# ScalarE takes the second square of the MLP; a shorter warm-up, another queue for the first input tile, a halved last output, and new instruction orders

## The chip, the cores and the metric

The kernel runs on one NeuronCore of a Trainium2 chip. The metric is the device time of one execution in microseconds (us). The kernel before took 510.14 us, the median of three runs (510.87, 508.67 and 510.14).

## The reference

One step of a hybrid decoder layer over T = 320 tokens: a prompt of 256, and 8 samples with 8 new tokens each. The model width is 1024 and everything is in f32. The layer is a sum of three residual branches, each behind an rmsnorm:

```python
def layer(x, pos, k_past, v_past, conv_buf, h0, mem_k, mem_v, lp):
    hn = rmsnorm(x, lp['ln_mix_g'])
    proj = hn @ lp['w_in']
    ...
    att = moba_attention(q, k_all, v_all, pos).reshape(b, t, ATT_WIDTH)
    xbc_c, new_conv = causal_conv(xbc, conv_buf, lp['conv_w'], lp['conv_b'])
    ...
    y, h_new = ssd_scan(xs, dt, a, bm, cm, h0)
    y = gated_group_norm(y, z, lp['ssm_norm_g'])
    x = x + jnp.concatenate([att, y], axis=-1) @ lp['w_out']
    x = x + cross_attn(rmsnorm(x, lp['ln_x_g']), mem_k, mem_v, lp)
    hm = rmsnorm(x, lp['ln_mlp_g'])
    x = x + jnp.square(jax.nn.relu(hm @ lp['w_up'])) @ lp['w_down']
    return x, k, v, new_conv, h_new
```

Of these the change touches the start (the rmsnorm ahead of `w_in` and the first product), the MLP (`w_up` is 1024 x 4096, `w_down` 4096 x 1024), and the last piece of the output.

## The kernel before

**Products.** Every weight is streamed from HBM in chunks of 128 x 1024 f32. A chunk is loaded into `wr` (3 buffers; L341, a DMA issued on SyncE's queue, or on ScalarE's for some of the chunks), and split into two fp32r halves that TensorE can multiply: `wh`, a rounded copy made by ScalarE (L393), and `wl`, the rest, a subtraction on VectorE (L394); both have 3 buffers. The activations are split in the same way, and each product is three matmuls, high by high, low by high and high by low (`gemm3`, L399, L400, L401). So a chunk with eight tiles of 128 rows gives 24 matmuls of 128 x 320.

**Stages.** In-projection with QK-norm and rotary, paged attention, convolution and state-space scan, output projection; cross-attention to the memory; then the MLP, with 32 chunks of `w_up` (each makes one tile of the 4096 hidden rows) and 32 of `w_down` (four make one of the eight output tiles).

**Start.** GpSimd clears a zero tile `ts` (L544), on which TensorE does warm-up matmuls whose product nobody reads (L547; their widths are `NWARM`, L68, and each f32 matmul is two passes in the trace). The table `prm` (L346, on ScalarE's queue), the first tile of x (L344, SyncE) and the first half chunk of weights (L341, SyncE) are loaded meanwhile. `split` makes the two halves of each tile of x times the norm's gain in `prm`: ScalarE the high one (L539), VectorE the low one (L540). The first real product is L719.

**The MLP's hidden rows.** When the 24 matmuls of a hidden tile are done, `up_done` (L1687 to L1696) takes them out of PSUM: t = max(product, 0) times the norm's factor `rb` (VectorE, L1692), hh = t squared, rounded to fp32r (ScalarE, L1693), f = t squared in f32 (GpSimd, L1695), hl = f - hh (VectorE, L1696). `t` and `f` come from one pool of five buffers. The product lies in one of two PSUM buffers `mm`, which comes free when L1692 has read it; a few tiles at the start of the stage, before `rb` is there, lie in `as` too. The output tiles of the MLP are added to x2T on VectorE (L1355, in `residual`) and go out by a DMA on SyncE (L1739).

**Order.** Nothing is scheduled at run time. TensorE's order comes from the string ORDER, in which each letter lets one generator (a part of a stage) emit its next piece; V and F are parts of the start, `u` and `w` two groups of hidden tiles, `r` the MLP's norm factor. The orders of ScalarE, VectorE, GpSimd and of the DMAs are four lists of numbers, ACT_ORDER, DVE_ORDER, POOL_ORDER and DMA_ORDER (runs of indices into the program order), which `_issue_order` applies at the end. Each engine works through its own list strictly in order: an instruction that waits holds up all behind it on that engine.

Of the kernel before, what the change touches and what calls it, by code (L numbers as in the profile page):

```python
# [12 lines left out]
AF = mybir.ActivationFunctionType  # L13
ALU = mybir.AluOpType
# [6 lines left out]
T = TP + NB * TS  # L21
# [26 lines left out]
for _n, _c in (("g_mix", 8), ("g_x", 8), ("g_mem", 8), ("g_mlp", 8), ("g_ssm", 4),  # L48
# [16 lines left out]
AHEAD = 2000  # L65
AHEAD2 = 400
AHEAD3 = 600
NWARM = (512, 512, 352)  # L68
PACE = 1.3
ORDER = ("VFVVVQQQQQQQQQQQQQQVQFVQFQVFQFQQQFVQQQQSSQQQFSSQQQZQZSSFSFSVSSQFFBBBBSZBSZBBSFBBTBBSSSBBBSSBBTBTBBTS"  # L70
         "SBSBBSSBSSSBSTSTBZSZBBSSBTBBZBBTSDBZSSDSSSTSZSZDDZTDSSZSDDSDDSDTDZZDDSDSZDDSZRSSSSSRRSRRSMOOROWRRWOR"
         "OWNOOWNONOOOOOMOONNOOWNJJJJJJJJJJMJZJJWJJKJKKKKKKKKKKKKKKKWGGOGGMaXcGJMGGGGGMGWGGGGGGMXXbcXaabcadcbc"
         "babbXaaMbccdadcdddacdGGGGGGKGGGGGWGGGGGG!uuuwuruuuuwwrwwwwuwuuuuuuuuuuuuuuuuuuuutuuuuuuuutuuutuuuuuu"
         "uuuuuuutuuutuuuuutuuutututuuuuuuutuuuuutuuuuuuuuuutuuuttuuutuuutuuutuuuuuuuuuuuuuuuuuuuu")
ACT_ORDER = ("1+3 20 5+1 19 21 7 0 8+2 22 11+3 16+1 23 15 24 28 30 33 18 27 25 32 26 29 38 34 43 37 31 50 39 36 57 44 35 "
# [15 lines left out]
DVE_ORDER = ("0+3 17 4+1 18 6+1 9 8 19 10 12 14+1 13 11 20+1 27 32 25 22 26 35 23 28 16 30 36 31 29 51 24 33 37 34 39+1 38 "  # L91
# [19 lines left out]
DMA_ORDER = ("1+2 0 4+11 19+1 16+2 21+1 29+4 23 34+1 24 36 28 37+5 45 43 46 44 47+6 64 54 25+1 55+3 65 59+2 27 66 62 75 67+4 "  # L111
# [5 lines left out]
POOL_ORDER = ("13 0+1 3 5 8 4 7 11 2 6 12 18 9+1 14 26 15+2 25 19+2 23+1 22 28 27 46 29 32 31 30 35+1 47 34 37 33 44 38+2 42 "  # L117
              "45 43 49 41 48 50+1 53 52 54+31")
TAKEN = []


# [135 lines left out]
def _body(tc, nc, I, O):  # L257
    V, A, G, S, PE = nc.vector, nc.scalar, nc.gpsimd, nc.sync, nc.tensor
# [34 lines left out]
    def tm(n, dt=F32):  # L293
        return tl(tp_, [P, n], "t", dt, bufs=NT)
# [34 lines left out]
    xT, ay = xa[:, 0], xa[:, 1]  # L329
# [10 lines left out]
            c = HALVES[part] if part is not None else slice(0, 1024)  # L340
            last_load[:] = [(A if WSP <= i < WACT and ahead else S).dma_start(raws[i][:, c], I["w"][i][:, c]).ins]  # L341

    def load_x_tile(a, b):
        S.dma_start(xT[:, a:b, :], I["xT"][:, a:b, :])  # L344

    A.dma_start(prm[:, 0:8], I["prm"][:, 0:8])  # L346
    for kt in range(4):
        load_x_tile(kt, kt + 1)
        load(CH["v"] + kt // 2, False, kt % 2)
    load_x_tile(4, 6)  # L350
    load_x_tile(6, 8)
# [1336 lines left out]
    def up_done(m):  # L1688
        def done(ps):
            hh, hl = mlp["h"]  # L1690
            t = tm(T)
            V.scalar_tensor_tensor(t, ps[:, :T], 0.0, mlp["rb"], op0=ALU.max, op1=ALU.mult)  # L1692
            A.activation(hh[:, m, :], t, AF.Square)  # L1693
            f = tm(T)
            G.tensor_tensor(f, t, t, op=ALU.mult)  # L1695
            V.tensor_tensor(hl[:, m, :], f, hh[:, m, :], op=ALU.subtract)  # L1696
        return done

# [29 lines left out]
    xT = x2T[0]  # L1728
    hh, hl = mlp["h"]

    for m in range(8):
        ps = mm()
        for c in range(4):
            w = chunk(CH["dn"] + 4 * m + c)
            for k in range(8):
                kt = 8 * c + k
                gemm3(ps[:, :T], w, slice(k * P, k * P + P), hh[:, kt, :], hl[:, kt, :], kt == 0, kt == 31)
        residual(m, None, None, None)(ps)
        S.dma_start(O["yT"][:, m, :], xT[:, m, :])  # L1739
    for take, runs in ((lambda i: i.engine == mybir.EngineType.Activation, ACT_ORDER), (lambda i: i.engine == mybir.EngineType.DVE, DVE_ORDER),  # L1740
                       (lambda i: i.engine == mybir.EngineType.Pool, POOL_ORDER),
                       (lambda i: i.opcode == "DMACopy", DMA_ORDER)):
# [32 lines left out]
```

## Time and profile before

| | before |
|---|---|
| runs, us | 510.87, 508.67, 510.14; median 510.14 |
| the profiled execution's own time, us | 510.33 |
| its span, first to last instruction, us | 508.5 |
| PE busy, share of the span | 98% |
| DVE busy | 66% |
| ACT busy | 50% |
| POOL busy | 11% |
| mean granted TensorE clock | 1.00 |

Times in the profile count from the first instruction. PE is TensorE's matmuls, PEld its weight loads, DVE VectorE, ACT ScalarE, POOL GpSimd and SP SyncE. A row of the timeline gives start, duration, engine, line, operation, output<-inputs and the number of instructions; in square brackets stands how long the engine was idle before it and what released it. Rows with a q (ACTq, SPq) are the engine's own queue issuing a DMA. "xN" rows join N neighbours. Matmuls overlap in the array, so their durations (0.31 us for 128 x 320) are longer than the distance from start to start.

### The profile page before, as it was taken

The page shows a single profiled execution, that of the slowest core. Times are in us where ns is not written, and L with a number is a line of the kernel's source. Part 1 is how long each engine was busy: PE and PEld are TensorE (multiplying, and loading weights), DVE is VectorE, ACT ScalarE, POOL GpSimd, SP SyncE. Part 2 cuts the span into 40 slices and gives each one's busy share as a digit, 9 for nine tenths or more (in the row PEclk, how much of TensorE's full clock was granted, in tenths as well). Part 3 has the DMA queues.
Part 4 walks back from the last instruction along what each step waited for, and adds up shares of the span by engine and source line. Part 5 has one row for each costly group of instructions (what it writes and reads, how often), then busy time and mean ns, then how long its engine had stood idle before and what let it go on. Part 6 is the DMA issues. An engine that isn't in the chain of part 4 may idle for free.

```text
span 508.5 us, 10447 instructions
## 1 busy us (share of the span) xinstructions
PE 499.4 (98%) x3954; PEld 454.5 (89%) x3954; DVE 335.8 (66%) x680; ACT 252.3 (50%) x520; POOL 56.8 (11%) x90
## 2 busy tenths in 40 slices
PE   8999999999999999999999999999999999999997
PEld 5988787878676899998799989999999999999997
DVE  5957899687596898776659568874865443433431
ACT  7634546959766855735666343342444332332230
POOL 1700101020100000000000223231333000000000
PEclk9999999999999999999999999999999999999999
DMA  8899999999999147877803474562663451746430
GB/s 289 307 369 356 341 377 363 323 351 351 350 382 356 64 167 249 261 300 257 341 5 122 158 290 133 179 219 100 224 191 124 153 193 59 258 111 209 160 112 13
DMA packets 45365, 116.53 MB, mean 229 GB/s; under 512 B 5059, under 2 KB 7235, under 8 KB 45315
## 3 DMA queue, kind: packets, MB, share of 16 engines
q1 hardware_dynamic: 39266, 94.37, 53.6%
q10 hardware_dynamic: 6048, 21.50, 11.9%
q8 instruction: 31, 0.51, 0.4%
q14 instruction: 20, 0.16, 0.1%
HBM read 109.71 MB, written 6.14 MB: 228 GB/s over the span
## 4 chain that ended last, share of the span: by engine, by line
PE 82%; DMA 7%; DVE 6%; ACT 2%; issue 1%; SPq 1%; ACTq 0%; POOL 0%; DVEq 0%
PE mm L399 21%; PE mm L400 20%; PE mm L401 20%; DMA wr<-w 3%; DMA kv<-ckT 3%; PE sc L881 3%; PE as L935 2%; PE ms L377 2%; DVE wl L394 2%; PE as L377 1%; PE sc L1555 1%; DMA kv<-cv 1%; PE ms L1657 1%; PE as L1579 1%; PE sc L1556 1%
## 5 line engine op out<-in xcount | busy, mean ns | idle before, releaser
L393 ACT ACTIVATE wh<-wr 128x1024 fp32r<-128x1024 f32 (+1 forms) x115 | 118.7, 1035 | 144.3 <-PE mm L400 97.7
L394 DVE TENSOR_TENSOR wl<-wr,wh 128x1024 fp32r<-128x1024 f32 (+1 forms) x115 | 140.4, 1228 | 64.8 <-ACT wh L393 63.1
L399 PE MATMUL mm<-big,wh 128*128 128x320 f32 x528 | 167.2, 317 | 1.6 <-DVE t L1692 1.6
L400 PE MATMUL mm<-big,wh 128*128 128x320 f32 x528 | 163.2, 309 | 0.1
L401 PE MATMUL mm<-big,wl 128*128 128x320 f32 x528 | 163.2, 309 | 0.0
L399 PEld LDWEIGHTS mm<-big,wh 128*128 128x128 f32 x528 | 99.1, 188 | 10.5 <-issue 8.3
L400 PEld LDWEIGHTS mm<-big,wh 128*128 128x128 f32 x528 | 99.2, 188 | 1.1 <-DVE big L1289 0.6
L401 PEld LDWEIGHTS mm<-big,wl 128*128 128x128 f32 x528 | 99.1, 188 | 0.1
L401 PE MATMUL mm<-hh,wl 128*128 128x320 f32 x256 | 78.9, 308 | 0.0
L400 PE MATMUL mm<-hl,wh 128*128 128x320 f32 x256 | 78.9, 308 | 0.0
L399 PE MATMUL mm<-hh,wh 128*128 128x320 f32 x256 | 78.9, 308 | 0.0
L1695 POOL TENSOR_TENSOR t<-t 128x320 f32<-128x320 f32 x32 | 34.4, 1077 | 158.2 <-DVE t L1692 140.1
L399 PEld LDWEIGHTS mm<-hh,wh 128*128 128x128 f32 x256 | 48.0, 188 | 0.0
L401 PEld LDWEIGHTS mm<-hh,wl 128*128 128x128 f32 x256 | 48.0, 188 | 0.0
L400 PEld LDWEIGHTS mm<-hl,wh 128*128 128x128 f32 x256 | 48.0, 188 | 0.0
L1693 ACT ACTIVATE hh<-t 128x320 fp32r<-128x320 f32 x32 | 13.8, 461 | 30.8 <-DVE t L1692 30.7
L1692 DVE SCALAR_TENSOR_TENSOR t<-mm,rb 128x320 f32<-128x320 f32 x30 | 14.5, 484 | 18.9 <-PE mm L401 15.5
L1696 DVE TENSOR_TENSOR hl<-t,hh 128x320 fp32r<-128x320 f32 x32 | 18.2, 596 | 12.8 <-ACT hh L1693 9.9
L1355 DVE TENSOR_TENSOR x2T<-mm,x2T 128x320 f32<-128x320 f32 x8 | 3.9, 488 | 21.1 <-PE mm L401 21.1
L881 PE MATMUL sc<-kv,qs 128*32 128x256 f32 x256 | 16.9, 382 | 0.2
L935 PE MATMUL as<-kv,p 128*32 128x256 f32 x256 | 15.3, 382 | 0.4 <-ACT p L921 0.4
L1008 DVE SCALAR_TENSOR_TENSOR t<-t,cwh,t 128x320 f32<-128x320 f32 x24 | 13.2, 550 | 3.2 <-ACT t L1005 1.8
(375 smaller groups left out, 648.1 us busy)
## 6 DMA issues: line engine op xcount, KB each, us to landing
wr<-w SPq DMA_DIRECT2D x69, 512.0 KB, 4.1
wr<-w ACTq DMA_DIRECT2D x41, 512.0 KB, 5.7
kv<-ckT SPq DMA_DIRECT2D x64, 256.0 KB, 5.4
kv<-cv SPq DMA_DIRECT2D x64, 256.0 KB, 6.2
kv<-mk SPq DMA_DIRECT2D x8, 512.0 KB, 5.4
kv<-mv SPq DMA_DIRECT2D x8, 512.0 KB, 5.9
kv<-h SPq DMA_DIRECT2D x4, 512.0 KB, 7.3
big<-h SPq DMA_DIRECT2D x4, 512.0 KB, 6.0
```

The source lines that it names most:

```text
L377: PE.transpose(out, in_, ident[:n, :n])
L393: A.activation(hi[:, c], raw[:, c], AF.Copy)
L394: V.tensor_tensor(lo[:, c], raw[:, c], hi[:, c], op=ALU.subtract)
L399: PE.matmul(out, hi[:, cols], xh, start=start, stop=False)
L400: PE.matmul(out, hi[:, cols], xl, start=False, stop=False)
L401: PE.matmul(out, lo[:, cols], xh, start=False, stop=stop)
L881: PE.matmul(ps[r:r + 32, 256 * n:256 * n + 256], qs[:, s, g, b0 + e, :], kbs[e][:, :, 128 * (2 * g + s):128 * (2 * g + s) + 128], start=s ...
L935: PE.matmul(yv[r:r + 32, 0:256], pT[:, 2 * n + q, r:r + 32], vbs[e][:, q, 256 * g:256 * g + 256], start=n == 0 and q == 0, stop=first and ...
L1692: V.scalar_tensor_tensor(t, ps[:, :T], 0.0, mlp["rb"], op0=ALU.max, op1=ALU.mult)
L1693: A.activation(hh[:, m, :], t, AF.Square)
L1695: G.tensor_tensor(f, t, t, op=ALU.mult)
L1696: V.tensor_tensor(hl[:, m, :], f, hh[:, m, :], op=ALU.subtract)
```

## The change

1. NWARM goes from (512, 512, 352) to (512, 512, 128).
2. `load_x_tile` gets a queue as an argument; the first tile of x is issued on ScalarE's queue instead of SyncE's.
3. f = t squared is an ACTIVATE with Square on ScalarE instead of a product on GpSimd, 32 times.
4. The last output tile (m = 7) is added and stored in two halves of 160 columns: the store of the first is on SyncE's queue, that of the second on ScalarE's.
5. ORDER, ACT_ORDER, DVE_ORDER, DMA_ORDER and POOL_ORDER are new.

```diff
-NWARM = (512, 512, 352)
+NWARM = (512, 512, 128)
...
-ORDER = ("VFVVVQQQQQQQQQQQQQQVQFVQFQVFQFQQQFVQQQQSSQQQFSSQQQZQZSSFSFSVSSQFFBBBBSZBSZBBSFBBTBBSSSBBBSSBBTBTBBTS"
+ORDER = ("FVVVVQQQQQQQQQQQQQQVQFVQFQVFQFQQQFVQQQQSSQQQFSSQQQZQZSSFSFSVSSQFFBBBBSZBSZBBSFBBTBBSSSBBBSSBBTBTBBTS"
...
-ACT_ORDER = ("1+3 20 5+1 19 21 7 0 8+2 22 11+3 16+1 23 15 24 28 30 33 18 27 25 32 26 29 38 34 43 37 31 50 39 36 57 44 35 "
+ACT_ORDER = ("2 1 0 4+1 3 21 6 20 7 22 8+2 12 11 13 23 14+1 17+1 16 24+1 29 31 26 34 28 33 19 30 35 39 27 44 38 32 51 40 45 "
...
-    def load_x_tile(a, b):
-        S.dma_start(xT[:, a:b, :], I["xT"][:, a:b, :])
-
+    def load_x_tile(a, b, q=S):
+        q.dma_start(xT[:, a:b, :], I["xT"][:, a:b, :])
+
+    load_x_tile(0, 1, A)
     A.dma_start(prm[:, 0:8], I["prm"][:, 0:8])
     for kt in range(4):
-        load_x_tile(kt, kt + 1)
+        if kt:
+            load_x_tile(kt, kt + 1)
         load(CH["v"] + kt // 2, False, kt % 2)
...
             A.activation(hh[:, m, :], t, AF.Square)
             f = tm(T)
-            G.tensor_tensor(f, t, t, op=ALU.mult)
+            A.activation(f, t, AF.Square)
             V.tensor_tensor(hl[:, m, :], f, hh[:, m, :], op=ALU.subtract)
...
-        residual(m, None, None, None)(ps)
-        S.dma_start(O["yT"][:, m, :], xT[:, m, :])
+        for q, c in ((S, slice(0, T)),) if m < 7 else ((S, slice(0, T // 2)), (A, slice(T // 2, T))):
+            V.tensor_tensor(xT[:, m, c], ps[:, c], xT[:, m, c], op=ALU.add)
+            q.dma_start(O["yT"][:, m, c], xT[:, m, c])
```

Line numbers of the changed kernel are 1 to 4 higher than those of before; below, its lines are named by those of before. TensorE's order changes in three places: the last warm-up matmul is narrower; one pair of transposes (L377) near the last sample attention stands about a dozen matmuls earlier; and at the start of the hidden rows the first tiles come in the order 0, 1, 2 where it was 0, 2, 1, so that the first two lie in `mm` and the third in `as`.

**ScalarE, start of the program, before.** `prm` is the gain table, `big_84` x, `big_116` its split high half, `wr` and `wh` the first chunk of weights as loaded and as copied, `t` the squares for the norm.

```order
L346 DMA prm_81<-prm 128x8
L539 ACT_TABLE_LOAD
L539 ACTIVATE big_116<-big_84,prm_81 128x320
L393 ACTIVATE wh_118<-wr_87 128x512
L539 ACTIVATE big_116<-big_84,prm_81 128x320
L487 ACTIVATE t_199<-big_84 128x320
L393 ACTIVATE wh_118<-wr_87 128x512
```

The same place in the changed kernel, where `tab` is one cleared column on which ScalarE does a first activation:

```order
L348 DMA prm_81<-prm 128x8
L345 DMA big_84<-xT 128x320
L325 ACT_TABLE_LOAD
L325 ACTIVATE tab_78<-tab_78 128x1
L396 ACTIVATE wh_118<-wr_87 128x512
L542 ACTIVATE big_116<-big_84,prm_81 128x320 x2
L490 ACTIVATE t_191<-big_84 128x320
L396 ACTIVATE wh_118<-wr_87 128x512
```

The load of x's first tile has come into this queue. The table load stood at the first use of x and `prm`; now it stands ahead of the activation on `tab`. The copy of the weights' first half now comes ahead of both splits of x (program index 5, the second tile, and then 3, the first). On SyncE the queue begins with the half chunk of weights, and every load behind it stands one place further ahead. On GpSimd the order of the first clearings was v, tab, ts, wdt and is now tab, ts, wdt, qs, v; at the hidden rows GpSimd has no instructions left (57 instead of 90 in all).

**VectorE, the first hidden tiles, before.** `t` numbers tell the tiles apart; `mm` and `as` are the PSUM buffers, `rb3` the norm's factor, `hl` and `hh` the two halves of the hidden rows.

```order
L1692 SCALAR_TENSOR_TENSOR t_733_4042<-mm_717_3942,rb3_712_3916 128x320
L394 TENSOR_TENSOR wl_742_4077<-wr_740_4074,wh_741_4076 128x1024
L394 TENSOR_TENSOR wl_750_4126<-wr_748_4123,wh_749_4125 128x1024
L1696 TENSOR_TENSOR hl_710_3914<-t_732_4033,hh_709_3913 128x320
L1696 TENSOR_TENSOR hl_710_3914<-t_730_4027,hh_709_3913 128x320
L1692 SCALAR_TENSOR_TENSOR t_743_4092<-as_735_4048,rb3_712_3916 128x320
L394 TENSOR_TENSOR wl_756_4163<-wr_754_4160,wh_755_4162 128x1024
L1696 TENSOR_TENSOR hl_710_3914<-t_734_4045,hh_709_3913 128x320
L394 TENSOR_TENSOR wl_762_4200<-wr_760_4197,wh_761_4199 128x1024
L1692 SCALAR_TENSOR_TENSOR t_745_4116<-mm_739_4073,rb3_712_3916 128x320
```

The same place in the changed kernel:

```order
L1695 SCALAR_TENSOR_TENSOR t_731_4030<-mm_717_3936,rb3_712_3916 128x320
L397 TENSOR_TENSOR wl_742_4077<-wr_740_4074,wh_741_4076 128x1024
L1695 SCALAR_TENSOR_TENSOR t_733_4042<-as_724_3982,rb3_712_3916 128x320
L397 TENSOR_TENSOR wl_750_4126<-wr_748_4123,wh_749_4125 128x1024
L397 TENSOR_TENSOR wl_756_4163<-wr_754_4160,wh_755_4162 128x1024
L1699 TENSOR_TENSOR hl_710_3914<-t_730_4027,hh_709_3913 128x320
L1695 SCALAR_TENSOR_TENSOR t_743_4092<-as_735_4048,rb3_712_3916 128x320
L1699 TENSOR_TENSOR hl_710_3914<-t_732_4033,hh_709_3913 128x320
L1699 TENSOR_TENSOR hl_710_3914<-t_734_4045,hh_709_3913 128x320
L397 TENSOR_TENSOR wl_762_4200<-wr_760_4197,wh_761_4199 128x1024
L1695 SCALAR_TENSOR_TENSOR t_745_4116<-mm_739_4073,rb3_712_3916 128x320
```

The instructions ahead of the last row are the same ones, but for one more L1692 at the front; what has moved is that two reads of PSUM stand a split of weights earlier or later, and the subtractions `hl` come in the order in which the tiles are squared. On ScalarE the two squares of a tile now stand mostly ahead of the next chunk's copy: behind the factor `rb3` come f, f, hh and a copy of weights, where one of weights, then another, and three hh stood.

More of the change, by code (lines that the diff above doesn't have):

```diff
@@ L67 @@
 AHEAD3 = 600
-NWARM = (512, 512, 352)
+NWARM = (512, 512, 128)
 PACE = 1.3
-ORDER = ("VFVVVQQQQQQQQQQQQQQVQFVQFQVFQFQQQFVQQQQSSQQQFSSQQQZQZSSFSFSVSSQFFBBBBSZBSZBBSFBBTBBSSSBBBSSBBTBTBBTS"
-         "SBSBBSSBSSSBSTSTBZSZBBSSBTBBZBBTSDBZSSDSSSTSZSZDDZTDSSZSDDSDDSDTDZZDDSDSZDDSZRSSSSSRRSRRSMOOROWRRWOR"
+ORDER = ("FVVVVQQQQQQQQQQQQQQVQFVQFQVFQFQQQFVQQQQSSQQQFSSQQQZQZSSFSFSVSSQFFBBBBSZBSZBBSFBBTBBSSSBBBSSBBTBTBBTS"
+         "SBSBBSSBSSSBSTSTBZSZBBSSBTBBZBBTSDBZSSDSSSTSZSZDDZTDSSZSDDSDDSDTDZZDDSDSZDDSZRSSSRSSRSRRSMOOROWRRWOR"
          "OWNOOWNONOOOOOMOONNOOWNJJJJJJJJJJMJZJJWJJKJKKKKKKKKKKKKKKKWGGOGGMaXcGJMGGGGGMGWGGGGGGMXXbcXaabcadcbc"
-         "babbXaaMbccdadcdddacdGGGGGGKGGGGGWGGGGGG!uuuwuruuuuwwrwwwwuwuuuuuuuuuuuuuuuuuuuutuuuuuuuutuuutuuuuuu"
-         "uuuuuuutuuutuuuuutuuutututuuuuuuutuuuuutuuuuuuuuuutuuuttuuutuuutuuutuuuuuuuuuuuuuuuuuuuu")
-ACT_ORDER = ("1+3 20 5+1 19 21 7 0 8+2 22 11+3 16+1 23 15 24 28 30 33 18 27 25 32 26 29 38 34 43 37 31 50 39 36 57 44 35 "
[15 rows of a table removed]
-DVE_ORDER = ("0+3 17 4+1 18 6+1 9 8 19 10 12 14+1 13 11 20+1 27 32 25 22 26 35 23 28 16 30 36 31 29 51 24 33 37 34 39+1 38 "
[19 rows of a table removed]
-DMA_ORDER = ("1+2 0 4+11 19+1 16+2 21+1 29+4 23 34+1 24 36 28 37+5 45 43 46 44 47+6 64 54 25+1 55+3 65 59+2 27 66 62 75 67+4 "
[5 rows of a table removed]
-POOL_ORDER = ("13 0+1 3 5 8 4 7 11 2 6 12 18 9+1 14 26 15+2 25 19+2 23+1 22 28 27 46 29 32 31 30 35+1 47 34 37 33 44 38+2 42 "
-              "45 43 49 41 48 50+1 53 52 54+31")
+         "babbXaacMbcdadcdddacdGGGGGGKGGGGGWGGGGG!uuwwurGuuuuwwruwwwuwuuuuuuuuuuuuuuuuuuuuuuuuuutuutuuutuuuuuu"
+         "uuuuuuutuuutuuuuutuuutututuuuuuuutuuuuutuuuuuuuuuutuuuttuututuuutuuuuuuuuuuuuuuuuuuuuuuu")
+ACT_ORDER = ("2 1 0 4+1 3 21 6 20 7 22 8+2 12 11 13 23 14+1 17+1 16 24+1 29 31 26 34 28 33 19 30 35 39 27 44 38 32 51 40 45 "
[16 rows of a table added]
+DVE_ORDER = ("1 0 2+2 17 5+1 18 7+2 19 10 12 14+1 13 20 11 27 32 25+1 35 21 16 22 28 30 36 51 23+1 33 31 34 37 29 39 38 40+6 "
[19 rows of a table added]
+DMA_ORDER = ("2+1 1 4+1 0 6+9 19+2 16+2 22 29+1 23 31+4 24 36+4 28 41+1 45 43+1 46+7 64 54+2 25+1 57+2 65 60+1 66 62 27 75 "
[5 rows of a table added]
+POOL_ORDER = ("0+1 3 12+1 2 5+1 8+1 14 11 4 7 10 18 15+2 19+3 24 23 26 25 27+2 31 30 32 34 36 46 35 47 37 33 44 49 39 38 40 "
+              "43 42 45 41 48 50+3")
 TAKEN = []
```

79 rows, old and new, of tables (ACT_ORDER, DMA_ORDER, DVE_ORDER) are left out of this document.

## The prediction

> **What bounds the kernel now.** I read the page's totals first, then what TensorE waits for, then the timeline at the start, at the hidden rows of the MLP and at the end. The totals:
>
> ```profile
> span 508.5 us, 10447 instructions
> PE 499.4 (98%) x3954; PEld 454.5 (89%) x3954; DVE 335.8 (66%) x680; ACT 252.3 (50%) x520; POOL 56.8 (11%) x90
> ```
>
> TensorE is busy for all but 9.1 us of the span, and the change takes no product away. So it can only fetch what TensorE loses: waits, the start, the end, and matmuls at a low clock. The list of TensorE's waits is complete:
>
> ```profile
> PE ms L547 <- POOL ts L544: 1.9, 1, 1.9
> PE mm L399 <- DVE t L1692: 1.6, 3, 0.8
> PE ms L377 <- ACT s L518: 0.6, 1, 0.6
> PE ms L377 <- DVE ts L620: 0.4, 2, 0.2
> PE as L935 <- ACT p L921: 0.4, 1, 0.4
> PE ms L1126 <- ACT ti L1162: 0.3, 1, 0.3
> PE ms L513 <- ACT sq L487: 0.2, 1, 0.2
> ```
>
> No wait for a DMA is among them: TensorE is ahead of no load after the start, so what the start gains is not handed back to HBM later. The first row is the start, the second the hidden rows, the other five (1.9 us) lie in attention, scan and norms. The start, on TensorE (first, seconds of the weight loads second), ScalarE and GpSimd:
>
> ```profile
> 1.93 4.95 PE L547 MATMUL ms<-ts 128*128 128x512 f32 x6 [1.93 <-POOL ts L544]
> 6.17 2.29 PE L719 MATMUL sc<-wh,big 128*128 128x512 f32 x4
> 8.29 0.63 PE L719 MATMUL sc<-wl,big 128*128 128x512 f32 x2
> 8.76 0.40 PE L719 MATMUL sc<-wh,big 128*128 128x512 f32 x1
> ```
>
> ```profile
> 4.65 0.34 PEld L547 LDWEIGHTS ms<-ts 128*128 128x128 f32 x1 [0.52 <-issue]
> 5.51 0.34 PEld L547 LDWEIGHTS ms<-ts 128*128 128x128 f32 x1 [0.52 <-issue]
> 6.09 0.34 PEld L719 LDWEIGHTS sc<-wh,big 128*128 128x128 f32 x1 [0.25 <-issue]
> ```
>
> ```profile
> 0.74 0.40 ACTq L346 DMA_DIRECT2D prm<-prm  x1
> 3.30 1.28 ACT L539 ACT_TABLE_LOAD   x1 [3.30 <-DMA prm<-prm]
> 4.60 0.56 ACT L539 ACTIVATE big<-big,prm 128x320 fp32r<-128x320 f32 x1
> 5.07 0.61 ACT L393 ACTIVATE wh<-wr 128x512 fp32r<-128x512 f32 x1
> 5.59 0.55 ACT L539 ACTIVATE big<-big,prm 128x320 fp32r<-128x320 f32 x1
> ```
>
> ```profile
> 0.74 0.52 POOL L585 MEMSET v<- 64x512 f32 x1 [0.29 <-POOLq L1767]
> 1.32 0.10 POOL L322 MEMSET tab<- 128x1 f32 x1
> 1.35 0.53 POOL L544 MEMSET ts<- 128x512 f32 x1
> ```
>
> TensorE stands for 1.93 us until the zero tile is cleared. A warm-up pass of 512 columns takes 0.85 (4.65 to 5.51), one of 352 takes 0.58 (5.51 to 6.09), and the second narrow pass holds the first real product to about 6.68, whatever its record's start of 6.17 says. Real matmuls run slowly until about 8.2: from 8.29 to 8.76 two of 512 columns start in 0.47, a full-clock distance of 0.235, while the four from 6.17 to 8.29, less the warm-up's last 0.51, took 0.40 each. So the clock turned up some 6.3 us after the first warm-up matmul. ScalarE is blocked too: its table load waits for `prm` until 3.30, though it needs no data.
>
> **The change part by part.** *Start.* Against these rows: the zero tile's clearing no longer stands behind that of v, so it is done 1.35 - 0.77 = 0.58 earlier, and the warm-up starts at 1.35. It has four passes of 0.85 (the first 1.0) and two of 0.58 x 128/352 = 0.21: it ends at about 1.35 + 3.57 + 0.43 = 5.35 instead of 6.68. Is the data there? The rows on the loads:
>
> ```profile
> 0.75 0.39 SPq L344 DMA_DIRECT2D big<-xT  x1
> ...
> 1.66 0.43 SPq L344 DMA_DIRECT2D big<-xT  x1
> ...
> big<-xT SPq DMA_DIRECT2D x4, 160.0 KB, 4.7
> ```
>
> In ScalarE's new order the table load waits only for the 0.10 us clearing of `tab` and two DMA issues of 0.40, so it ends near 2.9. Then come the weights' copy, x's second tile, x's first tile. The second tile is issued at 1.20 instead of 1.66, one SyncE issue ahead; it was in use at 5.59, so it landed at most 3.93 after its issue here, and at the soonest after 2.5 (that of `prm`, 0.74 to 3.30). It is there between 3.7 and 5.13, and with two splits of 0.55 the first product may begin between 4.8 and 6.2. I take 5.5, near the middle and just behind the warm-up's end: 1.18 earlier. Those matmuls run at half speed. If the clock turns after the same 6.3 us of work, at 7.62, TensorE has done by 8.2 (7.62 - 5.5)/2 + 0.58 = 1.64 us worth of full-clock work instead of (8.2 - 6.68)/2 = 0.76: gain 0.88. If it turns at the same moment: 1.35 - 0.76 = 0.59. Data at 6.2 leaves 0.24; TensorE free at 5.35 gives at most 0.96. I take -0.85, because the clock followed work and all loads move with it. x's first tile costs SyncE 0.45 less in every later load and ScalarE 0.40 under cover of its waiting.
>
> *Tail.*
>
> ```profile
> 505.19 0.49 DVE L1355 TENSOR_TENSOR x2T<-mm,x2T 128x320 f32<-128x320 f32 x1 [8.39 <-PE mm L401]
> 505.71 0.34 SPq L1739 DMA_DIRECT2D out_yT<-x2T  x1
> ```
>
> A half addition takes at least 0.25, so the first store leaves 0.25 earlier; the second leaves with the old one, or up to 0.3 later, with half its bytes. Between -0.3 and +0.3; I take -0.1.
>
> *The square on ScalarE.* Around the longest stall in the hidden rows, the timeline of TensorE and the groups of 285 to 400 us (the second VectorE fence: 405 to 505, the down half, where GpSimd does nothing):
>
> ```profile
> 295.69 0.31 PE L400 MATMUL mm<-big,wh 128*128 128x320 f32 x1
> 295.84 0.31 PE L401 MATMUL mm<-big,wl 128*128 128x320 f32 x1
> 296.95 0.39 PE L399 MATMUL mm<-big,wh 128*128 128x320 f32 x1 [0.80 <-DVE t L1692]
> ```
>
> ```profile
> L394 DVE TENSOR_TENSOR wl<-wr,wh 128x1024 fp32r<-128x1024 f32 x31 | 41.5, 1350 | 7.5 <-ACT wh L393 7.2
> L1696 DVE TENSOR_TENSOR hl<-t,hh 128x320 fp32r<-128x320 f32 x31 | 17.7, 600 | 8.5 <-ACT hh L1693 5.6 <-issue 2.1 <-POOL t L1695 0.8
> ```
>
> ```profile
> L394 DVE TENSOR_TENSOR wl<-wr,wh 128x1024 fp32r<-128x1024 f32 x27 | 32.8, 1223 | 44.9 <-ACT wh L393 44.9
> ```
>
> ```profile
> L1693 ACT ACTIVATE hh<-t 128x320 fp32r<-128x320 f32 x31 | 13.3, 461 | 30.8 <-DVE t L1692 30.7
> ```
>
> ```profile
> L1695 POOL TENSOR_TENSOR t<-t 128x320 f32<-128x320 f32 x32 | 34.4, 1077 | 158.2 <-DVE t L1692 140.1 <-ACT hh L1693 11.7 <-ACT wh L393 6.4
> ```
>
> ```profile
> 285.00:400.00 115.00, 113.41 (x786) 111.61 (x785) 79.92 (x110) 44.91 (x64) 34.38 (x32) 1.00 0.54 179
> ```
>
> TensorE waits because VectorE comes late to empty `mm`. VectorE's split is 1350 ns here and 1223 without GpSimd, its subtraction 600; of the same 128 x 320 shape the tail's addition took 490 (505.19 above). Without GpSimd's product VectorE thus gets 31 x 0.127 + 31 x 0.11 = 7.3 us of its 79.9 back, and 8.5 us of waiting ahead of the subtractions becomes shorter, since f no longer takes 1.08. The work ahead of the third read of `mm` in the order is the same as before, so that stall must go by these shorter times; a split and two subtractions give 0.127 + 2 x 0.11 = 0.35, the waiting ahead of them up to 8.5/31 = 0.27 each. The Trainium skill, SBUF — State Buffer, section Who interferes with whom, says that a VectorE instruction with two SBUF inputs contends with a GpSimd instruction that reads SBUF, while ScalarE never waits for anyone. The two means of the split bear the first part out; by the second, the move costs ScalarE nothing beyond its own time.
>
> ScalarE takes on 32 x 0.461 = 14.8 us, from 44.9 to 59.7 of 115: half idle still. The three waits sum to 1.6 us; in lost distance more, for from 295.84 to 296.95 are 1.11 where 0.15 is regular, 0.96 for a wait told as 0.80. So 1.6 x 1.2 = 1.9 is lost. I take -1.7: the two short ones go, the long one nearly. Bounds: -1.9, and, with ScalarE's squares in the way of the copies, a loss (rival D).
>
> *Other orders.* The narrow moves on TensorE, SyncE, ScalarE and VectorE elsewhere: 0, with the five middle waits (1.9) as bound below. Upward the same 1.9, as new waits of the same kind.
>
> Sum: -0.85 - 1.7 - 0.1 = -2.65. The profiled execution took 510.33 and lies 0.19 above the median, 1.83 outside its span; from 510.14 the forecast is **507.5**.
>
> **The rivals.** *C, the middle goes too.* The new orders were made for all engines, and the five waits sit on ScalarE and VectorE, whose lists are new. For it: those engines have idle time (66% and 50% busy). Against: TensorE's order is hardly new there, and a chain of dependences keeps its length. All five gone, by the same 1.2: -2.3, and the sum is -4.95: 505.2.
>
> *B, the waits move, the start is eaten.* A stall of the hidden rows goes only if `mm` is emptied in time at every tile; three others can replace the three, since VectorE keeps 73 us of work there. The start gives 0.24 if x's second tile is late. With a third of the stalls gone (0.3 to 0.6): 509.6.
>
> *E, the clock turns later.* If a hole opens between warm-up and first product, and the clock's count begins anew with the product, it turns at 5.5 + 6.3 = 11.8. By then 3.15 us worth is done, before it was 0.76 + 3.6 = 4.36: +1.2 at the start, and with -1.8 for the rest 509.5. The Trainium skill, TensorE: Matmul & The Clock Gate, Part 1, says that the full clock comes after a sustained busy window of about 3.4 us, in windows that run free; an estimate by that page is one window later than 8.2, so 11.6, much the same time. Here one trace shows the turn once, without a hole.
>
> *D, slower: squares ahead of weight copies.* ScalarE's new order puts f and f and hh ahead of the copies. If TensorE is as near to its weights as it is to `mm`, each tile whose copy is held by one more square costs 0.46. Sixteen of the 32: +7.4, the old 1.9 stays, less 0.95 at start and tail: 516.6. It decides from (0.95 + 2.55)/0.46, about 8 tiles. Against it: ScalarE waits 30.7 us for t in this stage, TensorE waits for no `wh` or `wl` anywhere, and three buffers of each stand between.
>
> **How the numbers follow.** Forecast 0.43, C 0.22, B 0.20, E 0.05, D 0.10. A measurement of this kernel can tell about 0.5%, 2.55 us, from no change: faster is below 507.6, slower above 512.7. The forecast lies on the first bound, so half of its chance is on either side: faster 0.22 + 0.23 = 0.45; slower is D, 0.10; the rest 0.45. The range leaves out D and a little on either side: from C with the best start and tail (505.2 - 0.6), 504.6, to B with the three runs' scatter above its 509.6, 511.2.
>
> **What would show it.** In the changed profile: the first warm-up near 1.35; the first L719 weight load near 5.3; the clock's turn near 7.6; no wait on L1692, L394 near 1.22 and L1696 near 0.49 us in the hidden rows; ScalarE busy about 60 of 115 us there. C shows by missing waits at L377, L935 and L1126. D would show as waits of L399 for ScalarE's copy or VectorE's split in the hidden rows; E as distances of 0.43 at 10 us. The forecast is wrong if TensorE's waits are longer than about 3 us in sum after 10 us, or if its busy time, corrected for the start, changes.

## The result and the profile after

The changed kernel took 506.57 us (median of six runs, 505.9 to 507.86) beside 509.84 for the kernel before (six runs, 508.67 to 511.17): ratio 0.9943, interval 0.9929 to 0.9957, so 3.27 us faster. It lies inside the range, 0.9 below the forecast of 507.5. The profiled execution is the slowest of the six, 507.86, and that matters below.

The page's totals of the changed kernel, and TensorE's waits:

```profile
span 506.1 us, 10434 instructions
PE 499.0 (99%) x3954; PEld 454.6 (90%) x3954; DVE 329.7 (65%) x681; ACT 264.3 (52%) x552; POOL 18.6 (4%) x58
```

```profile
PE ms L550 <- POOL ts L547: 1.4, 1, 1.4
PE sc L722 <- ACT big L542: 0.6, 1, 0.6
PE ms L380 <- ACT s L521: 0.6, 1, 0.6
PE as L938 <- ACT p L924: 0.4, 1, 0.4
PE ms L1129 <- ACT ti L1165: 0.3, 1, 0.3
PE ms L380 <- DVE ts L623: 0.2, 1, 0.2
PE ms L380 <- PE as L938: 0.2, 1, 0.2
```

The 1.6 us of waiting for VectorE in the hidden rows (L1692, now L1695) are gone, and the first row fell from 1.9 to 1.4. GpSimd has 58 instructions left (57 was said above). But a row has come that was not there: the first product (L722) waits 0.6 us for x's split. The start in the changed kernel, on TensorE:

```profile
1.35 4.21 PE L550 MATMUL ms<-ts 128*128 128x512 f32 x6 [1.35 <-POOL ts L547]
6.15 2.08 PE L722 MATMUL sc<-wh,big 128*128 128x512 f32 x4 [0.60 <-ACT big L542]
8.03 1.05 PE L722 MATMUL sc<-wl,big 128*128 128x512 f32 x2
8.88 0.63 PE L722 MATMUL sc<-wh,big 128*128 128x512 f32 x1
9.31 0.63 PE L722 MATMUL sc<-wl,big 128*128 128x512 f32 x1
9.73 0.89 PE L722 MATMUL sc<-wh,big 128*128 128x512 f32 x2
10.46 0.39 PE L722 MATMUL sc<-wl,big 128*128 128x512 f32 x1
10.69 0.39 PE L722 MATMUL sc<-wh,big 128*128 128x512 f32 x1
10.93 0.40 PE L725 MATMUL as<-wh,kv 128*128 128x512 f32 x1
```

and on ScalarE with its queue:

```profile
0.74 0.41 ACTq L348 DMA_DIRECT2D prm<-prm  x1
1.18 0.46 ACTq L345 DMA_DIRECT2D big<-xT  x1
1.67 1.28 ACT L325 ACT_TABLE_LOAD   x1 [1.67 <-PEq L1771]
2.97 0.20 ACT L325 ACTIVATE tab<-tab 128x1 f32<-128x1 f32 x1
3.90 0.63 ACT L396 ACTIVATE wh<-wr 128x512 fp32r<-128x512 f32 x1 [0.73 <-DMA wr<-w]
5.09 1.01 ACT L542 ACTIVATE big<-big,prm 128x320 fp32r<-128x320 f32 x2 [0.55 <-DMA big<-xT]
```

The table load came early, as forecast (1.67 to 2.95), and then ScalarE waited for data twice: 0.73 for the weights and 0.55 for x. The first product began at 6.15 behind a hole of 0.6 us. The 512-column matmuls then start 0.42 to 0.43 apart up to 9.73 (8.88 to 9.31, 9.31 to 9.73) and 0.23 apart from 10.46 on: in this execution the clock turned near 10.3, where it turned near 8.2 in the first profile of before. The hidden rows, 285 to 400 us, on VectorE and ScalarE, and the busy times:

```profile
L397 DVE TENSOR_TENSOR wl<-wr,wh 128x1024 fp32r<-128x1024 f32 x33 | 40.3, 1222 | 14.9 <-ACT wh L396 14.8
L1699 DVE TENSOR_TENSOR hl<-t,hh 128x320 fp32r<-128x320 f32 x32 | 15.2, 487 | 5.8 <-ACT hh L1696 3.8 <-ACT t L1698 2.0
```

```profile
L1698 ACT ACTIVATE t<-t 128x320 f32<-128x320 f32 x32 | 14.5, 463 | 24.8 <-DVE t L1695 24.8
```

```profile
285.00:400.00 115.00, 115.00 (x801) 113.91 (x800) 76.16 (x113) 58.31 (x98) 0.00 (x0) 1.00 0.56 184
```

TensorE is busy for all 115 us. The split is back at its 1222 ns, the subtraction at 487, and ScalarE is busy for 58.3 us. The tail:

```profile
502.49 0.31 PE L404 MATMUL mm<-hh,wl 128*128 128x320 f32 x1
502.83 0.56 DVE L1742 TENSOR_TENSOR x2T<-mm,x2T 128x160 f32<-128x160 f32 x2 [8.39 <-PE mm L404]
503.19 0.34 SPq L1743 DMA_DIRECT2D out_yT<-x2T  x1
503.42 0.35 ACTq L1743 DMA_DIRECT2D out_yT<-x2T  x1
```

**Where the time went, matmul by matmul.** TensorE's order is nearly the same in both kernels and both traces have all 3954 matmuls, so the start of the n-th can be set against the n-th of before's first profile. Where the warm-up has two matmuls fewer (e8_short), they are counted from the last one. The table gives what each stretch became longer or shorter by (us): the start up to the 41st matmul (14.97 in before), the middle up to the 2454th (284.69), the hidden rows up to the 3240th (400.12), and the tail from the last matmul's start to the end. The down half in between differs by 0.00 in all.

| kernel | start | middle | hidden rows | tail | span |
|---|---|---|---|---|---|
| changed (the profile above) | +0.80 | -0.85 | -2.31 | -0.13 | 506.06 |
| changed, second profile (e1_again) | -1.07 | -0.69 | -2.31 | -0.14 | 504.34 |
| changed, third (e11_again2) | -1.02 | -0.29 | -2.31 | -0.13 | 504.80 |
| before, second profile (e10_before) | -0.79 | +0.17 | -0.54 | 0.00 | 507.39 |
| f on GpSimd (e3_f_gpsimd) | +1.01 | -0.83 | -1.04 | -0.14 | 507.55 |
| warm-up 352 (e2_warm352) | -1.14 | -0.70 | -2.31 | -0.14 | 504.27 |
| x first (e7_x_first) | -1.25 | -0.83 | -2.31 | -0.14 | 504.03 |
| old start (e5_old_start) | -0.37 | -0.33 | -2.31 | -0.14 | 505.40 |
| short warm-up (e8_short) | +0.96 | -0.75 | -2.31 | -0.13 | 506.32 |
| last tile whole (e6_whole) | -1.18 | -0.68 | -2.31 | 0.00 | 504.39 |
| x first, warm-up 352 (e9_x_warm) | -1.41 | +0.25 | -2.31 | -0.14 | 504.95 |
| warm-up 352 again (e12_warm352_again) | -0.99 | -0.71 | -2.31 | -0.14 | 504.40 |
| third warm-up of 512 (e13_warm512) | -1.48 | -0.89 | -2.31 | -0.14 | 503.73 |

The start of one and the same kernel differs by 1.9 us between profiles, its middle by 0.6; the hidden rows of the changed kernel by nothing. The middle can be cut further: from the 181st to the 2201st matmul (36.92 to 254.26 us in before) all twelve profiles with the new orders are 0.56 to 0.67 shorter, and the second profile of before is 0.04 longer. What differs from run to run lies ahead of that piece and behind it.

### The profile page after: what moved, and what is told of

Read it like the earlier page. It is cut to its first block, busy times and chain, and to the rows that moved or that the text cites. A ratio compares the mean times of both kernels' runs of the same rounds, so it can differ in the third digit from the quotient of the medians.

```text
span 506.1 us, 10434 instructions
## 1 busy us (share of the span) xinstructions
PE 499.0 (99%) x3954; PEld 454.6 (90%) x3954; DVE 329.7 (65%) x681; ACT 264.3 (52%) x552; POOL 18.6 (4%) x58
## 4 chain that ended last, share of the span: by engine, by line
PE 92%; ACT 3%; DVE 3%; DMA 1%; issue 0%; SPq 0%; ACTq 0%; DVEq 0%
PE mm L402 23%; PE mm L403 23%; PE mm L404 23%; PE as L938 3%; PE sc L722 3%; PE ms L380 2%; PE sc L884 2%; PE as L380 1%; PE sc L1558 1%; DMA big<-xT 1%; PE ms L1660 1%; PE as L1582 1%; PE sc L1559 1%; PE mm L1632 1%; PE sc L1560 1%; PE as L1606 1%
## 5 line engine op out<-in xcount | busy, mean ns | idle before, releaser
L397 DVE TENSOR_TENSOR wl<-wr,wh 128x1024 fp32r<-128x1024 f32 (+1 forms) x115 | 137.0, 1194 | 78.5 <-ACT wh L396 77.5
L1698 ACT ACTIVATE t<-t 128x320 f32<-128x320 f32 x32 | 14.5, 463 | 24.8 <-DVE t L1695 24.8
L1695 DVE SCALAR_TENSOR_TENSOR t<-mm,rb 128x320 f32<-128x320 f32 x30 | 14.6, 488 | 17.0 <-PE mm L404 13.6
L1699 DVE TENSOR_TENSOR hl<-t,hh 128x320 fp32r<-128x320 f32 x32 | 15.2, 487 | 5.8 <-ACT hh L1696 3.8
L1742 DVE TENSOR_TENSOR x2T<-mm,x2T 128x320 f32<-128x320 f32 (+1 forms) x9 | 4.0, 450 | 19.5 <-PE mm L404 19.5
```

Of the source, the lines that this page charges most:

```text
L397: V.tensor_tensor(lo[:, c], raw[:, c], hi[:, c], op=ALU.subtract)
L1698: A.activation(f, t, AF.Square)
```

## The experiments

**f back on GpSimd, all else as changed.**

```diff
-            A.activation(f, t, AF.Square)
+            G.tensor_tensor(f, t, t, op=ALU.mult)
```

ScalarE's list loses the 32 entries, GpSimd's ends with them.

> The changed kernel with f = t squared back on GpSimd; all orders, start and tail as changed. Theory 'GpSimd's square slows VectorE and makes TensorE wait for mm': the splits are near 1.35 us again in the hidden rows, TensorE's waits for L1695 come back, and the time is 1.5 to 2.3 above the changed kernel, 508.1 to 508.9. Rival 'the new orders removed the stalls': no such wait, and 506.6 +/- 0.4.

Measured: 507.48 us (506.95 to 509.32), ratio to before 0.9964, interval 0.9953 to 0.9976, beside 506.17 and 0.9943 for the changed kernel in the same comparison. VectorE's groups in the hidden rows, and two rows of TensorE's waits:

```profile
L396 DVE TENSOR_TENSOR wl<-wr,wh 128x1024 fp32r<-128x1024 f32 x33 | 43.9, 1339 | 12.2 <-ACT wh L395 12.2
L1698 DVE TENSOR_TENSOR hl<-t,hh 128x320 fp32r<-128x320 f32 x31 | 18.0, 592 | 4.1 <-ACT hh L1695 2.4 <-POOL t L1697 1.8
```

```profile
PE mm L401 <- DVE t L1694: 0.6, 1, 0.6
PE mm L403 <- DVE wl L396: 0.2, 1, 0.2
```

The long durations are back (1339 and 592 ns), and with them a wait for `mm`; the table has 1.27 of the 2.31 us lost again. So the move of f is worth 1.3 us, 1.1 (0.21% of before) to 1.3 (of the medians) in the times, less than the 1.5 to 2.3 expected, and the other 1.0 is there without it: each theory has about half. The two short waits of before's first profile were these:

```profile
304.50 0.39 PE L399 MATMUL mm<-big,wh 128*128 128x320 f32 x1 [0.27 <-DVE t L1692]
327.64 0.39 PE L399 MATMUL mm<-big,wh 128*128 128x320 f32 x1 [0.53 <-DVE t L1692]
```

Set against the changed kernel, f on GpSimd loses 0.85 at the long wait near 297, where before lost 1.04, and 0.42 near 327, where TensorE now waits for a split of weights (0.16) instead of `mm`; near 304.5 nothing is lost, where before lost 0.51. How the durations make the long wait can be seen on VectorE, first with f on GpSimd, then in the changed kernel:

```profile
292.53 1.01 DVE L1698 TENSOR_TENSOR hl<-t,hh 128x320 fp32r<-128x320 f32 x1
293.86 1.40 DVE L1698 TENSOR_TENSOR hl<-t,hh 128x320 fp32r<-128x320 f32 x2
```

```profile
292.12 0.48 DVE L1699 TENSOR_TENSOR hl<-t,hh 128x320 fp32r<-128x320 f32 x1
292.92 0.89 DVE L1699 TENSOR_TENSOR hl<-t,hh 128x320 fp32r<-128x320 f32 x2
```

With f on GpSimd VectorE has no idle time from 290.25 until it reads `mm` at 296.32, so it is not f's later arrival that holds it there; the three subtractions alone are 1.04 longer. The two long ones, from 292.53 and from 294.26, run beside products on GpSimd (291.66 to 293.19 and 294.11 to 294.92); the one between them, from 293.86, has one beside it only in its last 0.23 and took 0.48.

**The changed kernel again, with no edit.**

> The changed kernel, unchanged, for a second profile and more times. If the hole of 0.6 us between warm-up and first product is what delays the clock, the second profile has the same hole and the distance of 512-column matmuls falls from 0.43 to 0.23 us near 10 us again, and the median is 506.6 +/- 0.5. If the moment of the turn is chance from run to run, it falls elsewhere between 7 and 11 us in this profile, with the same hole.

Measured: 506.17 us (505.86 to 506.87), ratio 0.9943, interval 0.9927 to 0.9959. TensorE at its start:

```profile
1.35 4.21 PE L550 MATMUL ms<-ts 128*128 128x512 f32 x6 [1.35 <-POOL ts L547]
6.03 1.34 PE L722 MATMUL sc<-wh,big 128*128 128x512 f32 x4 [0.47 <-ACT big L542]
7.21 0.62 PE L722 MATMUL sc<-wl,big 128*128 128x512 f32 x2
7.67 0.40 PE L722 MATMUL sc<-wh,big 128*128 128x512 f32 x1
```

From 6.03 to 7.21 four matmuls start, 0.30 apart on the mean, then 0.23 apart: the clock turned near 6.5, nearly 4 us earlier than in the first profile, with nearly the same hole (0.47), and earlier than the second case had allowed for (7 to 11). The prediction's count of 6.3 us of work does not hold: the moment varies from run to run.

**The kernel before again, with no edit.**

> The kernel before, for a second profile. If the clock turns at the end of a free-running stretch of some 3.4 us that was busy, the turn lies anywhere between 3.2 and 6.8 us after the first warm-up matmul at 1.93, without a hole, and the start may end up to 1.4 earlier than in the first profile. If it is a count of 6.3 us of work, as the prediction took it, the turn is at 8.2 again.

Measured: 509.15 us, one run, span 507.4. Its start is 0.79 shorter than in the first profile, for the clock had turned when the first product began: its matmuls start 0.23 apart from 6.4 on. Its waits for `mm`:

```profile
PE mm L399 <- DVE t L1692: 1.1, 2, 0.8
```

Two instead of three. The wait near 304.5 is still there:

```profile
303.87 0.39 PE L399 MATMUL mm<-big,wh 128*128 128x320 f32 x1 [0.26 <-DVE t L1692]
```

The one near 327 did not come in this execution, which makes the 0.54 of the table. So of the 1.04 us that stay gained without the move of f, 0.54 is a wait that before has only in some executions; 0.5 is left for the orders, and it is the wait near 304.5, which both profiles of before have and the kernel with f on GpSimd in the new order has not.

**A longer warm-up, twice.**

```diff
-NWARM = (512, 512, 128)
+NWARM = (512, 512, 352)
```

> The changed kernel with the old warm-up width (last matmul 352 columns). The warm-up then ends near 1.35 + 3.57 + 2 x 0.58 = 6.1, just when x's tiles are split, so there is no hole. Theory 'the hole delays the clock': the turn comes at 7.6 to 8.2, the first L725 matmul starts near 10.2 instead of 10.93, and the median is 0.7 below the changed kernel, 505.9. Rival 'the moment is chance': no difference beyond 0.3, 506.6. Rival 'the first product starts late': the start is at 6.15 or later and nothing is won.

> The changed kernel with the old warm-up width a second time. Theory: no hole while the clock is low, so no late runs: median 506.0, none above 506.7. Rival: as the changed kernel, 506.4 with late runs.

Measured: 505.97 us (505.92 to 506.49), ratio 0.9938, interval 0.9923 to 0.9953, and in the second comparison 506.20 (506.17 to 507.6), ratio 0.9945, interval 0.9931 to 0.9959. In the first profile the clock turned during the warm-up itself, which then ended early and left a hole of 0.59 at full clock, and the first product still waited for x until 5.96. The first comparison looked like the theory; the second had two runs of 507.5 and 507.6, which the theory had ruled out (neither of them has a profile). No difference from the changed kernel can be measured.

**A third warm-up matmul of 512 columns.**

```diff
-NWARM = (512, 512, 128)
+NWARM = (512, 512, 512)
```

> The changed kernel with a third warm-up matmul of 512 columns. Theory: no late runs either; where the clock turns late, the warm-up ends at 6.6 and holds the product by 0.45, worth 0.2 at half clock: median 506.0 to 506.2, none above 506.9. Rival 'a longer warm-up costs its own length': 506.8.

> The changed kernel a third time, beside the two kernels with a longer warm-up on the same chip. Theory 'the hole sometimes puts the turn off by one stretch': median 506.4, some of the runs 1 to 1.8 above the others. Rival: no difference to the next two.

Measured: 506.80 us (505.52 to 507.53), ratio 0.9948, interval 0.9936 to 0.9961; the unchanged changed kernel beside it 506.23 (506.11 to 506.85), ratio 0.9937, interval 0.9924 to 0.9951. The runs go from 505.52, the fastest of all, to three above 507. The profile, which is of the fastest run, has no hole; the late ones have no profile. At the low clock this warm-up ends only near 6.6 by the estimate above, behind x's split, so by this estimate a small hole at low clock is not what made them late: the theory gets no support here, though no trace of a late run refutes it. The unchanged kernel's five runs lie within 0.74 of each other, so the 1 to 1.8 expected for some of them did not come either.

**A much shorter warm-up.**

```diff
-NWARM = (512, 512, 128)
+NWARM = (512, 128)
```

> The changed kernel with two warm-up matmuls (512 and 128 columns) in place of three: the warm-up ends near 3.65 and TensorE stands for some 2.5 us until the first product at 6.1. Theory 'the clock turns at the end of a stretch of some 3.4 us that was busy nearly all the time, stretches that run free of the program': no stretch ahead of 6.1 counts, so the turn always comes between 9.5 and 13, the start ends about as late as in the changed kernel's first profile or up to 1.4 later, and the median is 1.0 to 1.8 above the changed kernel's, 507.4 to 508.2. Rival 'it needs a few us of work in sum, holes or not': 506.6 to 507. Rival 'the turn is unrelated to the warm-up': 506.4.

Measured: 508.12 us (507.75 to 508.87, ten runs), ratio 0.9977, interval 0.9968 to 0.9986. TensorE at its start:

```profile
1.35 2.50 PE L550 MATMUL ms<-ts 128*128 128x512 f32 x4 [1.35 <-POOL ts L547]
5.90 2.07 PE L722 MATMUL sc<-wh,big 128*128 128x512 f32 x4 [2.04 <-ACT big L542]
...
9.47 1.06 PE L722 MATMUL sc<-wh,big 128*128 128x512 f32 x2
10.33 0.63 PE L722 MATMUL sc<-wl,big 128*128 128x512 f32 x1
10.76 0.47 PE L722 MATMUL sc<-wh,big 128*128 128x512 f32 x1
11.06 0.40 PE L725 MATMUL as<-wh,kv 128*128 128x512 f32 x1
```

A warm-up so much shorter, with a hole of 2 us behind it, does cost: from 10.33 to 10.76 the matmuls are still 0.43 apart, and all ten runs are at least 1.1 above the changed kernel's median of 506.57. The rival "unrelated" falls, and so does "work in sum", which had 506.6 to 507. The shorter warm-up and the larger hole come together here and were not parted.

**x's first tile first, and its split first.**

```diff
-    load_x_tile(0, 1, A)
     A.dma_start(prm[:, 0:8], I["prm"][:, 0:8])
     for kt in range(4):
-        if kt:
-            load_x_tile(kt, kt + 1)
+        load_x_tile(kt, kt + 1)
...
-ACT_ORDER = ("2 1 0 4+1 3 21
+ACT_ORDER = ("1 0 2+2 4 20
```

> The changed kernel with x's first tile back at the head of SyncE's queue, and its split ahead of the weights' copy on ScalarE; the short warm-up stays. Theory 'the load order of the change makes the first product late': x's first tile is there near 3.0, the weights near 4.1, so the first product starts when the warm-up ends, near 5.35, without a hole; with the clock turning at 7.6 to 8.2 the first L725 comes near 9.8 instead of 10.93, and the median is about 1.1 below, 505.5. Rival 'the clock's turn alone decides': it turns at 10 all the same, and only 0.4 is won. Rival 'x's second tile comes too late instead': a wait of about 0.5 behind the first six matmuls, nothing won.

Measured: 506.21 us (505.8 to 507.21), ratio 0.9945, interval 0.9928 to 0.9962. The first matmuls of the products:

```profile
4.83 1.17 PE L720 MATMUL sc<-wh,big 128*128 128x512 f32 x4
5.83 0.61 PE L720 MATMUL sc<-wl,big 128*128 128x512 f32 x2
6.73 0.49 PE L720 MATMUL sc<-wh,big 128*128 128x512 f32 x1 [0.28 <-ACT wh L394]
7.45 0.50 PE L720 MATMUL sc<-wl,big 128*128 128x512 f32 x1 [0.23 <-DVE wl L395]
```

The first product comes 1.3 us earlier than in the changed kernel's first profile, and is then held at 6.73 and 7.45 by the second half chunk's copy and split. The last rival held in place and size, a wait of 0.51 in sum behind the first six matmuls. What TensorE waits for are the weights, but their copy stands on ScalarE behind the split of x's second tile, for which ScalarE waited until 5.23. Over the whole start nothing measurable is won.

**That order with the longer warm-up.** The two edits above together.

> x's first tile first on SyncE and split first, together with the old warm-up width of 352: no hole at any phase of the clock. Theory 'the hole costs through the clock': the turn comes at 8.2 at the latest, the slowest runs go, and the median is 505.9 with no run above 506.7. Rival 'the longer warm-up now delays the product': 506.4 and up.

Measured: 506.42 us (505.88 to 506.73), ratio 0.9940, interval 0.9928 to 0.9953. No gain over the changed kernel. In its profile the start is 1.41 shorter than before's, but the middle is 0.25 longer, where the others gain: TensorE waits 0.5 us for VectorE's sums at the norm's matmul at 28.97 (L508 here, L507 of before, where it does not wait).

**The whole start of before.** Warm-up of 352, x first on SyncE, the table load behind `prm`, v cleared first, the old order of splits; the rest as changed.

```diff
-ACT_ORDER = ("2 1 0 4+1 3 21 6 20 7
+ACT_ORDER = ("1+3 4 20 5 19 6 21 7 0
...
-POOL_ORDER = ("0+1 3 12+1 2
+POOL_ORDER = ("13 0+1 3 12 2
```

> The changed kernel with the whole start of before: warm-up of 352, x's first tile first on SyncE's queue, the table load behind the gain table, GpSimd clearing v first, the old order of the splits. Theory 'the start gives nothing on the mean': before less what the stages gave in the traces (hidden rows 2.3, middle 0.75, tail 0.14) is 509.5 - 3.2 = 506.3, the same as the changed kernel within 0.3. Rival, the prediction's term: the new start is worth 0.85 and this kernel comes to 507.2. In its profile the middle shows whether the 0.75 there came with the earlier loads of the start (then it is gone) or with the orders (then it stays).

**The last tile whole**, in the same comparison:

```diff
-        for q, c in ((S, slice(0, T)),) if m < 7 else ((S, slice(0, T // 2)), (A, slice(T // 2, T))):
+        for q, c in ((S, slice(0, T)),) if m < 8 else ():
```

> The changed kernel with the last output tile added and stored whole, on SyncE. Theory: the stretch from the last matmul's start to the last instruction is 3.71 us again instead of 3.57, and the time rises by 0.14, too little for the times to show. Rival 'two half stores are worth 0.3': the stretch is 3.87.

Measured: 506.72 us (506.33 to 507.71) with the old start, ratio 0.9950, interval 0.9939 to 0.9962; 506.46 (506.16 to 507.98) with the whole last tile, ratio 0.9952, interval 0.9939 to 0.9965. The tail theory holds in the trace: 0.00 instead of -0.14 against before. The old start lies between the theory's 506.3 and the rival's 507.2: the two kernels differ by 0.26 in their medians and hardly in their ratios. So the times show no more than some tenths from the new start, where the prediction had 0.85, but with intervals as wide as these they don't settle it. The middle is 0.33 shorter with the old start. The piece from 36.92 to 254.26 keeps its whole gain there (-0.64), so that one came with the orders; the difference lies ahead of it, where TensorE waits 0.39 for a split of weights at 34.73.

## Why the prediction was right, and where its steps failed

The forecast's direction and size came out right, but its first two terms were off, in opposite ways, and a third was left at zero that was not. That the sum came within 0.9 us is in part luck.

*Hidden rows: -1.7 forecast, -2.31 measured* against the first profile of before, -1.77 against the second. The mechanism was the one named: without GpSimd's product VectorE's split is at 1222 and its subtraction at 487 ns, and `mm` is emptied in time. It is shown by putting f back. The Trainium skill's rule, SBUF — State Buffer, section Who interferes with whom, that a VectorE instruction with two SBUF inputs contends with a GpSimd instruction that reads SBUF, is borne out: the same list of VectorE's instructions runs at 1339 and 592 ns beside GpSimd's product, and at 1222 and 487 without it. The step said that the long stall must go by the shorter times, since the work ahead of it is the same: 0.85 of its 1.04 come back with f on GpSimd. It missed two things. One is the size: the factor of 1.2 from wait to lost time came from the long stall, and the short ones lost 0.51 for a wait of 0.27 and 0.77 for one of 0.53. Where the step counted 0.11 for a subtraction, a mean over the stage, the three ahead of the long stall were 1.04 longer together. The other is the source: f's move is 1.27, the orders some 0.5 (the wait near 304.5, which goes without the move of f), and the wait near 327 comes and goes in before.

*ScalarE has room:* forecast 14.8 more and 59.7 of 115, measured 14.5 for f and 58.3. Rival D did not show: TensorE waits for no copy and no split in the hidden rows.

*Start: -0.85 forecast; about 0 in the profiles, some tenths in the times, not settled.* The mean of the start in the five profiles with the new start and an unchanged warm-up (+0.80, -1.07, -1.02, -1.18, and +1.01 with f on GpSimd) is -0.29; in the two of before (0 and -0.79) it is -0.40. With a spread of 2 us such means tell half a microsecond at best, so they show no gain, and they can't exclude one. Two steps failed. One is "I take 5.5" for the first product: it came at 6.15, 6.03 and 5.9 to 6.0, at the late end of the stated 4.8 to 6.2, because the copy ahead waited for its weights until 3.90 and both tiles of x waited until 5.09; x's first tile, which was there by 4.60 before, was now loaded behind others and split last. Emptying the path ahead of a load gains nothing where the load is what comes last. The other is "the clock followed work": the turn came 6.3 us after the first warm-up matmul in one execution of before, some 3.5 in the other (there the second narrow warm-up pass follows the first after 0.29, half of the 0.58 of the slow clock), and 9.0 (10.3 - 1.35) and 5.2 (6.5 - 1.35) in two of the changed kernel. The Trainium skill, TensorE: Matmul & The Clock Gate, Part 1, has the turn at the end of a busy window of about 3.4 us that runs free of the program; the scatter between profiles agrees with that, a fixed count doesn't. Rival E, with a hole and a late turn, is what the first profile shows, +0.8 at the start; but e1_again had nearly the same hole and an early turn, and the later comparisons did not tie the late runs to the small hole. What makes some runs 1 to 1.5 us later stays open; only the shorter warm-up with its hole of 2 us was shown to cost.

*Tail: -0.1 forecast, -0.14 measured*, shown by the whole tile.

*Other orders: 0 forecast, -0.29 to -0.85 measured* in the middle. The step that failed is the zero: the piece from 36.92 to 254.26 is some 0.6 shorter in every profile with the new orders, with the old start (-0.64) and with f on GpSimd (-0.58) too, and 0.04 longer in the second profile of before. So it is neither the start nor f's square, and the new orders are what is left. Rival C's signs did not show: the waits at L935, L1126 and for ScalarE at L377 are as long as before (0.4, 0.3 and 0.6), and that of L513 (0.2), gone in the changed kernel, is missing in the second profile of before as well. Of the two waits at L377 for VectorE one stayed at 0.2, and the other is put down to TensorE's own L935 now. About half of the gain, 0.32, lies between 161 and 169 us of before's trace, where the moved pair of transposes stands (24 matmuls earlier, not the dozen said above); that it is these transposes was not tried.

Together, from the means: +0.10 for the start, -0.75 for the middle (-0.67 in the same five profiles against +0.08 in the two of before), -2.04 for the hidden rows (-2.31 against -0.27), -0.13 for the tail: -2.8, beside -3.27 in the medians. The difference is within the scatter of the start. The range's upper bound lies 1.6 above rival B, more than the three runs' scatter above their median (0.73); nothing hangs on it.

## What to carry to other kernels

Where the bottleneck engine waits for few tenths at a time, cut the spans into stretches and set its n-th instruction in one trace against the n-th in the other: it told the terms of each profile here, to a hundredth, where the times could tell only the sum. Take two profiles or more of both kernels before explaining a term: starts differed by 1.9 us, and a wait in the hidden rows of before came and went. And when an engine takes over a step because another engine's copy slowed a third, count the third engine's own instructions: their durations were the largest part of what that move gained.

## What the runs showed of the hardware

TensorE's low clock at the start, told by the distance of 512-column matmuls (0.43 us against 0.23), ended between about 4.3 us (e2_warm352) and 10.9 us (e8_short), and before 6.0 (e11_again2) or near 10.3 in profiles of the changed kernel itself, whose starts differ by 1.9 us; the moments are estimates from these distances. The profile's column of the granted clock read 1.00 in the slices with half-speed matmuls: the distance of equal matmuls has to be read instead. A ScalarE square of 128 x 320 in f32 took 463 ns where GpSimd's product took 1077, and ScalarE's copies took 1056 ns on the mean before and 1054 after it. With f on GpSimd in the new order, VectorE's products of the state scan took 811 ns on the mean, and 684 in the changed kernel (128 x 512; L1250 of before).
